# In-projection: products 1 and 2 of all sixteen pairs ahead of the rest, on input that is not yet normalised; up-projection: begun pairs in turns, two products in one bank

## The chip, the cores and the metric

One core of a Trainium2 chip runs the kernel. The metric is the device time of one execution in microseconds (us). The kernel before was timed three times: 1247.93, 1248.74 and 1249.16 us, median 1248.74.

## The reference

One layer of an encoder trunk over 1024 tokens of width 1024, all in float32. What matters here is the first step, and that the same kind of product stands at two more places:

```python
h    = rms_norm(x, norm_mix_pre)            # x * rsqrt(mean(x*x)) * gain
proj = h @ w_in                             # 1024 x 1024 by 1024 x 4096
q, k, v, u, gates = split(proj, ...)
...                                         # attention, pooling, gates, W_o, residual
f = conv_gated_ffn(rms_norm(x), w_up, ...)  # rms_norm(x) @ w_up, 1024 x 5632, conv, GELU gate, @ w_down
x = x + rms_norm(f)
```

The root mean square is taken per token, so in `h @ w_in` it may be left out of the product and multiplied in afterwards, one factor for each token (`Rb` in the code); the gain is per channel of the inner dimension and has to be in before.

## The kernel before

**Products.** A float32 operand is split into a high part (rounded to fp32r, a cast on ScalarE, `wh` or a name with `h`) and the rest (a subtraction on VectorE, `wl` or `l`). A product of two split operands takes three matmuls: high by high, high by low, low by high (`mm3`, L82). All matmuls of the projections are 128x128 weights against 128x512 input columns into one bank of PSUM. One product of 512 inner channels is 4 x 3 = 12 matmuls.

**Pairs.** The output columns of a projection are worked in pairs of 128-column blocks: 16 pairs in the in-projection (`IN_PAIRS`), 22 in the up-projection. A pair is a product of a 2x2 matrix of blocks (two column blocks f by two halves of the inner dimension) and a 2x2 matrix of input quadrants (two halves of the inner dimension by two halves t of the tokens). Done directly it takes 8 products; `Pair` (L165) does it by Strassen and Winograd's scheme in 7: p1 and p2, whose sum is the block f=0, t=0, and then p5, p6, p3, p7, p4, which use sums of weights (`s1` to `s4`, on POOL from L204 to L210) and sums of input quadrants (`T1` to `T4`). p1 and p2 use plain weights (`w11`, `w12`) and plain quadrants (`B11`, `B21`), the first token half. The result of p1 (`c1`) is needed again: p6 accumulates on it in the same bank X.

**In-projection.** The first pairs are where the input comes in, is scaled by the gain and split. Pairs 0 and 1 are done directly, 8 products each (L414, 192 matmuls on four gain-scaled quadrants `XR`), and their results are multiplied by `Rb` at eviction (`evict_first`, L446). Meanwhile the sums of squares (`sq`, L424, ScalarE), the reciprocal roots (`scales`), the spread of them over the partitions by four transposes (`spread`, `rps`) and the normalisation of the four quadrants in place (`normalise`, L440) run. Pairs 2 to 15 then take 7 products each from the normalised quadrants. Pairs 4 and 5 are begun early: their p1 and p2 run in the `m` banks, `c1` is kept in SBUF, and their later products are evicted with an add of `c1` on VectorE (L217, L248, L485). In the others p6 adds to p1 in the bank, and the evictions of p1, p5 and p6 are ScalarE copies. The pool path (trailing means on VectorE) runs beside pairs 8 to 11.

**Up-projection.** Pairs 2, 3, 4 are begun early in the `m` banks: p1 to SBUF, p2 evicted with an add (L1158); both go to DRAM (`e_d`) and come back at the pair's turn, where p5, p6 and p4 are evicted with an add of `c1s`. The order of the begun products is written out by hand from L1218 to L1278.

**What sets the order.** Each engine takes its instructions in one order. The code gives it, a scheduler may move an instruction where a priority (`tc.high_priority`) or a hold (`tc.issue_after`) is set; loads are issued by SP, some stores by ScalarE (`sig_d`). PSUM has eight banks: tags X, Y, Z and m, two each.

Of the kernel before, what the change touches and what calls it, by code (L numbers as in the profile page):

```python
# [46 lines left out]
def trunk(ctx, tc, xn, xt, w_first, w_in, cols, gain_pre, bias, w_ao, w_pg, w_po, w_o, gains, w_up, w_dn, out):  # L47
# [20 lines left out]
    g_d = dram.tile([NG, P, S], F32, name="g_d")  # L68
    e_d = dram.tile([2, 3, P, 512], F32, name="e_d")
# [7 lines left out]
    def split(hi, lo, src, eng=None):  # L77
        r = A.copy(hi, src)  # L78
        (eng or V).tensor_tensor(lo, src, hi.bitcast(F32), ALU.subtract)  # L79
        return r  # L80
# [84 lines left out]
    class Pair:  # L165
# [3 lines left out]

        def __init__(self, raw, T, psp, tmp, name, evict, np_=6, eng=G):  # L170
            self.early, self.eng, self.split = False, eng, {}
            self.weights(raw)
            self.T, self.psp, self.tmp, self.name, self.evict, self.np_ = T, psp, tmp, name, evict, np_
# [38 lines left out]
        def p5(self):  # L212
# [3 lines left out]
            if self.early:  # L216
# [4 lines left out]
        def begin(self, w, c1):  # L221


            self.early, self.c1 = True, c1
            w = w.rearrange("p (q k c) -> p q k c", q=2, k=4)
            self.w11, self.w12 = w[:, 0], w[:, 1]

        def p1(self):
            if self.early:
                self.X = self.bank("m")  # L230
# [4 lines left out]
            A.copy(self.c1, self.X)  # L235

        def p2(self):
            Z = self.bank("m" if self.early else "Z")
# [3 lines left out]
        def p6(self):  # L242
# [3 lines left out]
            self.prod(self.X, self.s2, "T2", self.early, "6")  # L246
            if self.early:
# [15 lines left out]
        def p4(self, last):  # L263
            X, c = (self.bank("Z"), self.c7) if last else (self.X, self.c1 if self.early else None)
# [58 lines left out]


    mx = [[], []]


    with ExitStack() as ph:
# [13 lines left out]
        def out_tile(f, dt=F32):  # L342
            return tmp.tile([P, 512], dt, tag="hl", bufs=4, name=f)
# [4 lines left out]

        XR = {(0, 0): two("T1", "XR00")}
        xts = []
        for n, tag in enumerate(("B11h", "B11l", "B21h", "B21l")):
            x2 = Tp.tile([P, 2, D], F32, tag=tag, name=f"x{n}")
            xts += [x2[:, 0], x2[:, 1]]
        XR[1, 0] = two("T2", "XR10")
        sq = Tp.tile([P, D], F32, tag="B22h", name="sq")
        Tp.tile([P, D], F32, tag="B22l", name="b22l")
        XR[0, 1] = two("T3", "XR01")
        XR[1, 1] = two("T4", "XR11")  # L360

# [7 lines left out]
        A.dma_start(gn, gain_pre)  # L369
        for c in (slice(0, 1), slice(1, 2), slice(2, 4)):  # L370
            nc.sync.dma_start(q[0, 0][:, c], xt[0, 0][:, c])
            nc.sync.dma_start(wr[0][:, c], w_first[0][:, c])
        for c in (slice(0, 2), slice(2, 4)):
            nc.sync.dma_start(q[1, 0][:, c], xt[1, 0][:, c])
            nc.sync.dma_start(wr[1][:, c], w_first[1][:, c])
        for n in range(4):
            nc.sync.dma_start(xts[n], xn[n])
        for i in range(2):
            nc.sync.dma_start(q[i, 1], xt[i, 1])
        for n in range(4, 8):  # L380
            nc.sync.dma_start(xts[n], xn[n])
        nc.sync.dma_start(cv, cols)
# [8 lines left out]
        def split_raw(i, j, k):  # L391
            hi, lo = XR[i, j]
            A.activation(hi[:, k], q[i, j][:, k], AF.Identity, scale=gain(i, k))
            V.scalar_tensor_tensor(lo[:, k], q[i, j][:, k], gain(i, k), hi[:, k].bitcast(F32),
                                   ALU.mult, ALU.subtract)

        ws, acc = {}, {}

        def split_first(i, k):

            place = (lambda: tmp.tile([P, 2, 4, P], F32R, tag="o", name="w0s", bufs=4)) if i == 0 else None
            ws[i, k] = split_w(wr[i][:, k].rearrange("p (b c) -> p b c", b=4), f"first{i}{k}", None, place)

        def bank(b, t, tag):
            acc[b, t] = psp.tile([P, 512], F32, tag=tag, name=f"i_{b}{t}")

        def products(bs, t, i, k):


            wh, wl = ws[i, k]  # L410
            th, tl = XR[i, t]
            for p, (w, x) in enumerate(((wh, th), (wh, tl), (wl, th))):
                for b in bs:
                    nc.tensor.matmul(acc[b, t], w[:, b], x[:, k], start=i == k == p == 0,  # L414
                                     stop=i == 1 and k == 3 and p == 2, skip_group_check=True)
# [11 lines left out]
        def spread(j):  # L427
# [6 lines left out]
            Rb[j] = out_tile(f"R{j}")  # L434
# [7 lines left out]
        def evict_first(pi, t):  # L442
            for f in range(2):
                b = IN_PAIRS[pi][f]
                d = half_tile(f"d{b}_{t}")
# [1059 lines left out]
```

## Time and profile before

| | |
|---|---|
| median of three runs | 1248.74 us |
| the profiled execution | 1248.39 us |
| its span on the core | 1246.6 us |
| PE (matmul) busy | 1231.2 us, 99%, 5756 matmuls |
| VectorE (DVE) busy | 939.8 us, 75% |
| ScalarE (ACT) busy | 657.3 us, 53% |
| GpSimd (POOL) busy | 282.9 us, 23% |
| mean granted TensorE clock | 0.999 |

The profiled execution's time lies 1.8 us above its span, and 0.35 us below the median. The share of busy time is taken over the whole span; stages differ. Up to about 100 us the in-projection prepares its input beside its first products; its last p6 is at 323 us; the scores of the attention run from 332 to 460 us, the products behind it up to about 606 us; the up-projection has its last p6 at 1021 us, and the down-projection the rest.

### The profile page before, as it was taken

What the parts mean: (1) busy time and instruction counts of PE and PEld (TensorE: products, weight loads), DVE (VectorE), ACT (ScalarE), POOL (GpSimd) and SP (SyncE); (2) the same over time, 40 slices, a digit from 0 to 9 for tenths busy, and PEclk for the clock granted to TensorE, in tenths of its full rate; (3) what the DMA queues carried; (4) which work ended last, traced back from release to release, by engine and by line L of the source; (5) the groups of instructions that cost most, each with busy time, mean ns of one, the idle gap of its engine ahead of it and who ended that gap; (6) DMA issues with size and microseconds to landing.
All of it is one profiled execution on the core that took longest, in us unless ns stands there. A gap on an engine that the chain in (4) does not pass through costs nothing.

```text
span 1246.6 us, 16208 instructions
## 1 busy us (share of the span) xinstructions
PE 1231.2 (99%) x5756; PEld 1023.7 (82%) x5756; DVE 939.8 (75%) x1503; ACT 657.3 (53%) x1149; POOL 282.9 (23%) x229
## 2 busy tenths in 40 slices
PE   7999999999999999999999999999999999999997
PEld 6888888888889888888788888888888888888886
DVE  5996346876588887756799988666676676899968
ACT  6663345564487774434545555455545555445553
POOL 0004222232255546000003443334334300000000
PEclk9999999999999999999999999999999999999999
DMA  9336024335988746412344333122231216903103
GB/s 355 138 131 231 26 89 184 129 131 188 297 277 269 263 154 242 152 73 86 112 148 153 130 110 126 61 102 73 79 101 56 88 68 221 377 18 101 35 1 136
DMA packets 57329, 178.11 MB, mean 143 GB/s; under 512 B 5344, under 2 KB 5984, under 8 KB 52384
## 3 DMA queue, kind: packets, MB, share of 16 engines
q1 hardware_dynamic: 51264, 164.23, 37.3%
q10 hardware_dynamic: 4752, 8.39, 1.8%
q0 software_dynamic: 1232, 4.46, 0.9%
q8 instruction: 45, 0.74, 0.2%
q14 instruction: 36, 0.29, 0.1%
HBM read 128.30 MB, written 48.76 MB: 142 GB/s over the span
## 4 chain that ended last, share of the span: by engine, by line
PE 89%; DVE 8%; issue 1%; ACT 1%; DMA 0%; DVEq 0%; SPq 0%; ACTq 0%
PE X_u L86 16%; PE X_i L86 12%; PE Y_u L86 9%; PE X L86 7%; PE wops L1063 7%; PE Y_i L86 6%; PE i L414 4%; PE Z_u L86 4%; PE y L86 4%; PE ybp L86 4%; PE Y L86 3%; PE Z_i L86 3%; PE f L863 3%; PE tp L838 2%; PE m_u L86 2%; PE pst L795 2%
## 5 line engine op out<-in xcount | busy, mean ns | idle before, releaser
L1187 DVE SCALAR_TENSOR_TENSOR hc<-hu,cv,hc 128x1022 f32<-128x1022 f32 (+1 forms) x88 | 122.7, 1396 | 27.0 <-ACT hc L1182 26.8
L78 ACT CAST wh_u<-s_u 128x512 fp32r<-128x512 f32 x88 | 54.4, 619 | 92.4 <-PE X_u L86 41.7
L79 DVE TENSOR_TENSOR wl_u<-s_u,wh_u 128x512 fp32r<-128x512 f32 x88 | 66.5, 757 | 30.0 <-ACT wh_u L78 30.0
L79 DVE TENSOR_TENSOR wl_i<-s_i,wh_i 128x512 fp32r<-128x512 f32 x56 | 42.7, 763 | 37.3 <-ACT wh_i L78 37.1
L78 ACT CAST wh_i<-s_i 128x512 fp32r<-128x512 f32 x56 | 34.6, 622 | 59.9 <-PE X_i L86 21.9
L78 ACT CAST wh_u<-wup 128x512 fp32r<-128x512 f32 x60 | 37.3, 622 | 52.3 <-PE Y_u L86 27.3
L1182 ACT ACTIVATE hc<-hu,cv 128x1024 f32<-128x1024 f32 x44 | 54.6, 1244 | 12.2 <-DVE hu L1131 11.4
L208 POOL TENSOR_TENSOR s_u<-s_u,wup 128x512 f32<-128x512 f32 x19 | 26.6, 1403 | 131.1 <-DVE wl_u L79 131.1
L204 POOL TENSOR_TENSOR s_u<-wup 128x512 f32<-128x512 f32 x19 | 33.7, 1775 | 74.7 <-DVE wl_u L79 74.7
L204 POOL TENSOR_TENSOR s_i<-win 128x512 f32<-128x512 f32 x11 | 15.9, 1446 | 150.8 <-DVE wl_i L79 112.8
L817 POOL TENSOR_SCALAR pe<-pe,st 128x640 f32<-128x640 f32 (+4 forms) x58 | 40.3, 699 | 42.2 <-DVE st L815 28.3
L813 ACT ACTIVATE pe<-sm,st 128x640 f32<-128x640 f32 (+2 forms) x64 | 44.3, 694 | 8.1 <-DVE st L811 7.8
L79 DVE TENSOR_TENSOR ptl<-tp,pth 128x512 fp32r<-128x512 f32 (+3 forms) x80 | 43.0, 552 | 7.4 <-ACT pth L78 6.6
L210 POOL TENSOR_TENSOR s_u<-wup 128x512 f32<-128x512 f32 x19 | 40.7, 2141 | 27.2 <-DVE wl_u L79 27.2
L1192 ACT ACTIVATE hc<-hc 128x1024 f32<-128x1024 f32 x22 | 23.4, 1062 | 39.8 <-DVE hc L1187 39.8
L78 ACT CAST pth<-tp 128x512 fp32r<-128x512 f32 (+3 forms) x80 | 36.4, 474 | 14.8 <-PE tp L838 10.5
L86 PE MATMUL ybp<-mx,wh_yb 128*128 128x512 f32 x128 | 43.4, 414 | 0.0
L78 ACT CAST wh_i<-win 128x512 fp32r<-128x512 f32 x38 | 23.4, 622 | 37.4 <-PE X_i L86 22.8
L79 DVE TENSOR_TENSOR wl_u<-wup,wh_u 128x512 fp32r<-128x512 f32 x60 | 42.1, 702 | 0.7
L811 DVE CUSTOM_DVE_ANT_0 sm<-pst,bt 128x640 f32<-128x640 f32 (+2 forms) x64 | 40.5, 651 | 2.7 <-issue 1.5
L863 PE MATMUL f<-ptl,vv 128*128 128x256 f32 x144 | 36.5, 287 | 0.0
L838 PE MATMUL tp<-ident,pe 128*128 128x128 f32 x240 | 36.2, 275 | 0.1
(503 smaller groups left out, 4169.9 us busy)
## 6 DMA issues: line engine op xcount, KB each, us to landing
wup<-in_w_up SPq DMA_DIRECT2D x22, 1024.0 KB, 5.0
win<-in_w_in SPq DMA_DIRECT2D x14, 1024.0 KB, 5.8
g_d<-hc SPq DMA_DIRECT2D x20, 512.0 KB, 2.7
sig_d<-d ACTq DMA_DIRECT2D x32, 256.0 KB, 2.0
a<-g_d SPq DMA_DIRECT2D x8, 1024.0 KB, 10.9
b<-in_w_dn SPq DMA_DIRECT2D x8, 1024.0 KB, 12.3
x<-in_xn SPq DMA_DIRECT2D x8, 512.0 KB, 11.5
v_d<-vt SPq DMA_DIRECT2D x8, 512.0 KB, 3.1
```

The source lines that it names most:

```text
L78: r = A.copy(hi, src)
L79: (eng or V).tensor_tensor(lo, src, hi.bitcast(F32), ALU.subtract)
L86: nc.tensor.matmul(ps, a[i], b[i], start=start and i == 0 and p == 0, stop=stop and i == n - 1 and p == 2, skip_group_check=True,)
L204: self.eng.tensor_tensor(self.s1, self.w21, self.w22, ALU.add)
L210: self.eng.tensor_tensor(self.s3, self.w11, self.w21, ALU.subtract)
L414: nc.tensor.matmul(acc[b, t], w[:, b], x[:, k], start=i == k == p == 0, stop=i == 1 and k == 3 and p == 2, skip_group_check=True)
L813: A.activation(pe[:, :n], sm[:, :n], AF.Exp, scale=-1.0, bias=st[:, 0:1], accum_out=st[:, 1:2])
L838: nc.tensor.transpose(tp[:, c * P:(c + 1) * P], pe[:, b * P:(b + 1) * P], ident)
L863: nc.tensor.matmul(fo, vv[:, kb, e].rearrange("p a d -> p (a d)"), t[:, s], start=s == slots[0] and x == 0, stop=s == slots[-1] and x == 1)
L1063: nc.tensor.matmul(ps[:, 512 * c:512 * c + 512], a[k // 4][:, k % 4, sl], wo[k][b][:, 512 * c:512 * c + 512], start=k == 0 and x == 0, sto ...
L1182: A.activation(c, hu, AF.Identity, scale=cv[:, C_CW + 88 + b:C_CW + 89 + b], bias=cv[:, C_CB + b:C_CB + b + 1])
L1187: V.scalar_tensor_tensor(c[:, n:], hu[:, :S - n], cv[:, w:w + 1], c[:, n:], ALU.mult, ALU.add)
```

## The change

In the in-projection:

- Only two quadrants (first token half) are scaled by the gain and split, un-normalised (`XR` of two), and these are the operands `B11` and `B21` for all pairs.
- The first 96 matmuls are p1 (into banks X X Y Y) and p2 (into Z Z m m) of pairs 0 to 3 together. For pairs 4 to 15, p1 of pair n and p2 of pair n-1 alternate; p2 accumulates on p1 in one bank, and the tags X, Y, Z take turns. All 16 blocks f=0, t=0 are multiplied by `Rb[0]` at eviction, on VectorE.
- Each `c1` is copied out by ScalarE, stored to a new DRAM tensor (`c1_d`, 16 x 256 KB, issued by ScalarE) and loaded again at the pair's turn (by SP) into a single buffer.
- After that all 16 pairs take their other five products. Before p6, VectorE writes `c1` times `Rb[0]` into the X bank (a seed), and p6 accumulates on it, so p5, p6 and p4 are evicted without an add of `c1`. The pool path runs beside pairs 6, 8, 10, 12, the first two attention heads are loaded beside pair 14.
- The sums of squares, roots, spreads, normalisation and the operands `T1` to `T4`, `B22` are spread between the early products.

In the up-projection the order of the begun products becomes u1 p1, u1 p2, u2 p1, u3 p1, u2 p2, u4 p1, u3 p2, u4 p2, each p2 on its p1 in one bank (tags X, Y, X); the evictions of p2 and of their later p5 and p6 are ScalarE copies, and the X bank is seeded by a ScalarE copy.

```diff
 class Pair:
         def p1(self):
             if self.early:
-                self.X = self.bank("m")
+                self.X = self.bank(self.tags[0])
...
-            A.copy(self.c1, self.X)
+            with tc.high_priority() if self.tags != "mm" else nullcontext():
+                A.copy(self.c1, self.X)
 
         def p2(self):
+            if self.tags != "mm":
+                self.prod(self.X, self.w12, "B21", False, "2")
+                self.evict(0, 0, self.X, None)
+                return
             Z = self.bank("m" if self.early else "Z")
...
             if self.early:
                 self.X = self.bank("X")
-            self.prod(self.X, self.s2, "T2", self.early, "6")
-            if self.early:
+            if self.scale is not None:
+                V.tensor_tensor(self.X, self.c1, self.scale, ALU.mult)
+            elif self.seed:
+                A.copy(self.X, self.c1)
+            self.prod(self.X, self.s2, "T2", self.early and not self.seed, "6")
+            if self.early and not self.seed:
                 V.tensor_tensor(self.u2, self.X, self.c1, ALU.add)
             else:
                 A.copy(self.u2, self.X)
...
+        for n in range(5, NP):
+            if n + 3 < NP:
+                load_w12(n + 3)
+            if n == 6:
+                nc.sync.dma_start(q[1, 1], xt[1, 1])
+            p = begin(n)
+            with tc.high_priority():
+                p.prep("1", p.w11)
+            p.p1()
+            keep_p1(n)
+            with tc.high_priority():
+                p.prep("2", p.w12)
+            pairs[n - 1].p2()
+            if n == 9:
+                values()
+            for x in extra.get(n, ()):
+                x()
...
         def ahead(g):
 
-            p = Pair(None, Tu, psu, tmp, f"u{g}", None, 4)
+            p = Pair(None, Tu, psp, tmp, f"u{g}", None, 4)
...
             def evict(f, t, ps, add):
                 d = p.pt("p2")
-                V.tensor_tensor(d, ps, add, ALU.add)
+                A.copy(d, ps)
                 nc.sync.dma_start(e_d[0, g - 2], d)
```

**How the rows move.** In the rows below, `i7` is pair 7 of the in-projection and `u2` pair 2 of the up-projection; `wh_5_i7` and `wl_5_i7` are the high and low weights of its p5.

VectorE in the in-projection's regular stretch, around the turn from pair 6 to pair 7. Before:

```order
L79 TENSOR_TENSOR wl_7_i6_1244<-s3_i6_1124,wh_7_i6_1243 128x512
L485 TENSOR_TENSOR vd8_1204<-Z_i6_1187,p1_i6_1169 128x512
L79 TENSOR_TENSOR wl_5_i7_1270<-s1_i7_1206,wh_5_i7_1269 128x512
L79 TENSOR_TENSOR wl_4_i6_1287<-win6_956,wh_4_i6_1286 128x512
L485 TENSOR_TENSOR vd8_1204<-Y_i6_1128,u2_i6_1208 128x512
L79 TENSOR_TENSOR wl_1_i7_1308<-win7_1061,wh_1_i7_1307 128x512
L485 TENSOR_TENSOR vd9_1259<-X_i6_1168,p5_i6_1129 128x512
L79 TENSOR_TENSOR wl_2_i7_1326<-win7_1061,wh_2_i7_1325 128x512
L79 TENSOR_TENSOR wl_6_i7_1347<-s2_i7_1261,wh_6_i7_1346 128x512
L79 TENSOR_TENSOR wl_3_i7_1364<-s4_i7_1262,wh_3_i7_1363 128x512
```

VectorE at the same turn, now:

```order
L79 TENSOR_TENSOR wl_5_i7_1707<-s1_i7_1640,wh_5_i7_1706 128x512
L254 TENSOR_TENSOR X_i7_1787<-c1b_7_1638,R0_361 128x512
L79 TENSOR_TENSOR wl_4_i6_1724<-win6_1418,wh_4_i6_1723 128x512
L528 TENSOR_TENSOR d8_1_1678<-Y_i6_1596,u2_i6_1642 128x512
L79 TENSOR_TENSOR wl_6_i7_1790<-s2_i7_1698,wh_6_i7_1789 128x512
L528 TENSOR_TENSOR d9_1_1696<-X_i6_1643,p5_i6_1597 128x512
L79 TENSOR_TENSOR wl_3_i7_1807<-s4_i7_1699,wh_3_i7_1806 128x512
```

The splits of the weights of p1 and p2 and the add of p1 and p2 have gone from the turn; the seed (L254) has come, ahead of the split for p6 and behind that for p5.

VectorE at the second set of reciprocal roots (`bc1` is what `spread(1)` transposes). Before:

```order
L440 SCALAR_TENSOR_TENSOR xq10_105<-xq10_105,gn_112,R0_311 128x512
L309 TENSOR_SCALAR rs_a_339<-rs_a_339 128x4
L79 TENSOR_TENSOR B11l_488<-xq00_104,B11h_487 128x1024
L310 TENSOR_TENSOR rst_143<-rst_143,rs_a_339 128x4
L430 COPY bc1_404<-rst_143 128x512
```

VectorE there, now:

```order
L606 TENSOR_TENSOR d14_0_473<-Y_i5_370,R0_361 128x512
L319 TENSOR_TENSOR rs_a_410<-rs_a_410,rs_v_408 128x4
L478 SCALAR_TENSOR_TENSOR xq10_107<-xq10_107,gn_114,R0_361 128x512
L79 TENSOR_TENSOR wl_1_i8_535<-w12_8_363,wh_1_i8_534 128x512
L320 TENSOR_SCALAR rs_a_410<-rs_a_410 128x4
L478 SCALAR_TENSOR_TENSOR xq10_107<-xq10_107,gn_114,R0_361 128x512
L321 TENSOR_TENSOR rst_152<-rst_152,rs_a_410 128x4
L478 SCALAR_TENSOR_TENSOR xq10_107<-xq10_107,gn_114,R0_361 128x512
L79 TENSOR_TENSOR wl_2_i8_554<-w12_8_363,wh_2_i8_553 128x512
L468 COPY bc1_476<-rst_152 128x512
```

The four small steps of the roots now stand between evictions, splits and normalisations of 512 columns each, and `bc1` behind them.

ScalarE at the start of the up-projection. Before:

```order
L235 COPY hu1_1_6035<-m_u1_6055 128x512
L78 CAST B22h_6228<-h2_11_5214 128x1024
L78 CAST wh_1_u2_6069<-w12_2_6038 128x512
L78 CAST wh_2_u2_6087<-w12_2_6038 128x512
L78 CAST T1h_6112<-h2_00_5211 128x1024
```

ScalarE there, now:

```order
L238 COPY hu1_1_6116<-m_u1_6136 128x512
L79 CAST wh_1_u2_6150<-w12_2_6119 128x512
L79 CAST wh_2_u2_6169<-w12_2_6119 128x512
L79 CAST T1h_6193<-h2_00_5292 128x1024
L79 CAST wh_1_u3_6189<-w12_3_6122 128x512
```

The cast of `B22` no longer stands between the copy for pair 1 and the casts of the weights of pair 2; it follows further down, behind the copy of u2's p1.

More of the change, by code (lines that the diff above doesn't have):

```diff
@@ L570, in trunk @@
+        operand("T4", q[1, 0])
+        nxt.p6()
+        nxt.prep("3", nxt.s4)
+        nxt.p3()
+        pair.p7(False)
+        load_win(2)
+        load_win(3)
+        turn(2)
+        third.first()
+        nxt.p7(False)
+        third.sums()
+        pair.p4(False)
+        third.p5()
+        nxt.p4(False)
+        pair, pd = third, None
+        for pi in range(2, NP):
+            fb = IN_PAIRS[pi]
             for n in (pi + 1, pi + 2):
-                if n < len(IN_PAIRS) and n not in raws and pi >= 1 and (pi < 8 or n == pi + 1):
+                if n < NP and n not in raws and (pi < 9 or n == pi + 1):
```

427 lines of the change are left out of this document (195 added, 232 removed).

## The prediction

> **What bounds the kernel now.** I read the page first: the busy times, the granted clock and the chain that ended last.
>
> ```profile
> PE 1231.2 (99%) x5756; PEld 1023.7 (82%) x5756; DVE 939.8 (75%) x1503; ACT 657.3 (53%) x1149; POOL 282.9 (23%) x229
> PEclk9999999999999999999999999999999999999999
> PE 89%; DVE 8%; issue 1%; ACT 1%; DMA 0%; DVEq 0%; SPq 0%; ACTq 0%
> ```
>
> TensorE (PE) is busy for 1231.2 of 1246.6 us at full clock in every slice, so 15.4 us are idle in all. A busy PE need not be at its peak, so I look at a long stretch without a wait, and at stretches where another engine is full. In these rows of the windows view the columns are sum, PE (matmuls), weight loads, DVE, ACT, POOL, clock, DMA share, GB/s.
>
> ```profile
> 58.00:100.00 42.00, 42.00 (x187) 34.80 (x186) 41.71 (x54) 29.02 (x43) 0.01 (x1) 1.00 0.47 167
> 210.00:230.00 20.00, 19.58 (x86) 15.73 (x85) 15.07 (x21) 11.20 (x18) 6.10 (x4) 1.00 0.39 150
> 620.00:640.00 20.00, 20.00 (x89) 16.22 (x88) 19.82 (x26) 12.49 (x19) 0.00 (x0) 1.00 0.21 73
> 660.00:700.00 40.00, 39.11 (x172) 31.78 (x171) 39.85 (x40) 22.19 (x29) 16.85 (x8) 1.00 0.36 125
> 700.00:900.00 200.00, 200.00 (x884) 165.55 (x883) 149.03 (x169) 101.16 (x143) 73.11 (x45) 1.00 0.26 95
> ```
>
> Between 700 and 900 us, 884 matmuls of 512 columns follow each other without a gap: 200 / 884 = 0.2262 us each. A matmul less is 0.226 us less, as long as nothing else is late. DVE is full at 58 to 100 us and from 620 to 700 us; there the margin of what feeds PE is small. Then the waits of PE:
>
> ```profile
> PE i L414 <- ACT w0s L78: 6.7, 1, 6.7
> PE X_u L86 <- ACT wh_u L78: 0.5, 1, 0.5
> PE X_i L86 <- ACT u_i L250: 0.4, 1, 0.4
> PE X_u L86 <- DVE hu L1131: 0.4, 1, 0.4
> PE m_u L86 <- ACT wh_u L78: 0.3, 1, 0.3
> ```
>
> 6.7 us are the first load, 1.6 us are four waits in the two projections, and the rest of the 15.4 us, 7.1 us, lies in shorter gaps and behind the last matmul. So the bound is the number of matmuls; the waits that a change can remove are small.
>
> **The change part by part.**
>
> *Matmuls.* Pairs 0 and 1 took 8 products of 12 matmuls (the 192 of L414), now 7: 2 x 12 = 24 fewer, all of 128x512. All other pairs keep 7 products. 24 x 0.2262 = **5.4 us less**, on the path since PE is never waiting there. The Trainium skill's page TensorE: Matmul & The Clock Gate ("Wait — 56ns, not 53.3ns?") gives 512 columns 215.7 ns once warm; the row's 226 ns is longer and decides, and by the page's figure the term would be 5.2 us.
>
> *The start.* The first 96 matmuls use the same two quadrants, the same loads in the same order, and the same splits as now. I take no change for the 6.7 us and the cold matmuls.
>
> *First spread.* The roots of tokens 0 to 511 are now asked for behind p1 of pair 4 and ten matmuls of p1 of pair 5, at about 36.5 us (PE's own pace from the start). ScalarE has to do ahead of them, in its order: the copies of four `c1` and four issues, the casts for pairs 4 and 5, and four squares. The rows for these:
>
> ```profile
> L424 ACT ACTIVATE sq<-x 128x1024 f32<-128x1024 f32 x8 | 8.5, 1059 | 0.2
> L78 ACT CAST wh_i<-win 128x512 fp32r<-128x512 f32 x7 | 4.4, 623 | 7.1 <-PE i L414 4.2 <-PE X_i L86 2.7
> L440 DVE SCALAR_TENSOR_TENSOR xq<-xq,gn,R 128x512 f32<-128x512 f32 x16 | 11.4, 745 | 3.0 <-ACT R L435 3.0
> L462 DVE TENSOR_TENSOR xq<-xq,xq 128x1024 f32<-128x1024 f32 x8 | 9.5, 1221 | 0.0
> L446 DVE TENSOR_TENSOR d<-i,R 128x512 f32<-128x512 f32 x8 | 5.0, 681 | 0.0
> L430 DVE COPY bc<-rst x2: 427/428/428, 23.6 to 42.1; 128x512 f32<-128x512 f32 x2
> ```
>
> Four squares are 4.2 us by the row (and up to 0.8 us for reading their sums), five copies of 512 columns 3.1 us by the cast's row (same shape, so an upper bound), the four casts 2.5 us. With four issues of stores (an estimate, under 2 us) that is 10 to 12 us from the last split of the input at about 24 us: the root is out at about 35 us, and the small steps and `bc` follow in some 1.5 us. I take a new wait of 0.3 us, between 0 and 1.5.
>
> *Second spread.* Here DVE is in the way: in its new order the small steps of `bc1` stand between five normalisations, three splits and an eviction. Each costs DVE not its duration but the distance to the next; these rows of the timeline show both:
>
> ```profile
> 99.82 0.69 DVE L79 TENSOR_TENSOR wl_i<-win,wh_i 128x512 fp32r<-128x512 f32 x1
> 100.42 0.68 DVE L79 TENSOR_TENSOR wl_i<-s_i,wh_i 128x512 fp32r<-128x512 f32 x1
> 102.48 1.69 DVE L79 TENSOR_TENSOR wl_i<-s_i,wh_i 128x512 fp32r<-128x512 f32 x1 [1.38 <-ACT wh_i L78]
> 104.09 0.68 DVE L217 TENSOR_TENSOR p_i<-Y_i,c 128x512 f32<-128x512 f32 x1
> 104.69 1.46 DVE L79 TENSOR_TENSOR wl_i<-s_i,wh_i 128x512 fp32r<-128x512 f32 x1
> ```
>
> The second starts 0.60 us after the first, whose duration is 0.69. With 0.60 for a subtraction or product of 512 columns and, likewise 0.09 below its duration, 0.66 for a normalisation, `bc1` comes at about 50.9 us, as PE comes to `rps1` (eleven matmuls into p2 of pair 6). I take 0.2 us, between 0 and 2.4 (by whole durations).
>
> *The rest of the early phase.* PE does 28 products, 96 + 24 x 12 matmuls, up to about 99 us and then five products of pairs 0 and 1. DVE from the first normalisation (about 38.5 us) to the split that p6 of pair 1 needs has, counted in its order: 44 ops of 512 columns, 20 normalisations or scalings, 18 sums of 1024 columns (1.13 each, 1.22 - 0.09), 2 splits of the values, one `bc`, 6 small ones: 26.4 + 13.2 + 20.4 + 1.2 + 0.4 + 0.6 = 62.2 us. With some 8 us in which it waits for PE and ACT before 56 us (my own walk through its order), that ends at about 109 us; PE reaches p6 of pair 1 at about 110.1. No wait, with a margin of 1 to 1.5 us. This is the narrowest place of the change.
>
> *Seeds and c1.* DVE gets 16 seeds and 16 products by `Rb[0]`; it loses 12 adds of p1 and p2 and those of pairs 4 and 5. A turn is now 5 products, 5 x 12 x 0.226 = 13.6 us. Counted with the same prices, DVE has 4.8 us between two seeds for pairs 4 to 8, 10.6, 11.7, 7.4, 11.0, 4.4, 7.3 and 14.9 us before the seeds of pairs 9 to 15. The one above 13.6 follows two light ones, so no seed is late. The stores and loads of `c1_d` are 2 x 16 x 256 KB:
>
> ```profile
> sig_d<-d ACTq DMA_DIRECT2D x32, 256.0 KB, 2.0
> win<-in_w_in SPq DMA_DIRECT2D x14, 1024.0 KB, 5.8
> ```
>
> 256 KB land in 2.0 us, a turn is 13.6 us: hidden, also with one buffer. At SP each reload stands ahead of the next `win` (5.8 us); that is asked for a turn or more ahead. If the cover were gone, a late reload costs at most 2.0 us a turn.
>
> *Old waits of the in-projection.* The wait for `u_i` (0.4 us, in 210 to 230 us) is ScalarE's copy that p7 waits for; the copy stays. The pool path, which crowds ScalarE there (11.20 of 20 us), is now spread over twice as many pairs; I take 0.4 us less, between 0 and 0.4.
>
> *Up-projection.* Same number of matmuls. Three places are late there:
>
> ```profile
> 616.55 1.05 ACT L78 CAST B22h<-h 128x1024 fp32r<-128x1024 f32 x1
> 617.51 0.58 ACT L235 COPY hu<-m_u 128x512 f32<-128x512 f32 x1
> 617.98 1.05 ACT L78 CAST B22h<-h 128x1024 fp32r<-128x1024 f32 x1
> 618.93 1.14 ACT L78 CAST wh_u<-w 128x512 fp32r<-128x512 f32 x2
> 619.60 0.50 PE L86 MATMUL m_u<-B11h,wh_u 128*128 128x512 f32 x1 [0.32 <-ACT wh_u L78]
> 682.41 0.68 DVE L1131 TENSOR_TENSOR hu<-X_u,p_u 128x512 f32<-128x512 f32 x1
> 683.14 0.50 PE L86 MATMUL X_u<-T4h,wh_u 128*128 128x512 f32 x1 [0.41 <-DVE hu L1131]
> 688.57 1.68 POOL L210 TENSOR_TENSOR s_u<-wup 128x512 f32<-128x512 f32 x1 [0.63 <-DVE wl_u L79]
> 692.08 0.47 PE L86 MATMUL X_u<-T3h,wh_u 128*128 128x512 f32 x1 [0.48 <-ACT wh_u L78]
> ```
>
> At 619 us the cast for u2 stands behind 2 x 1.05 us of `B22`; in the new order it is in front of them. At 683 us p4 waits for an eviction on a full DVE; three adds of p2 and the first adds of u2 have gone to ScalarE by then, at least 4 x 0.60 = 2.4 us against a wait of 0.4. At 692 us the weights come late through a sum on POOL that waited for DVE (0.63 us), the same relief. The three waits are 0.32 + 0.41 + 0.48 = 1.2 us, and the first matmul behind each takes 0.47 to 0.50 us where one without a wait takes 0.39. I take 1.4 us less, between 0.3 and 2.0 (with the restarts counted). ScalarE has the time: 12.49 of 20 us and 22.19 of 40 us.
>
> *The sum*, from the profiled 1248.4 us: -5.4 (matmuls) + 0.3 + 0.2 (spreads) - 0.4 (old waits) - 1.4 (up-projection) = **1241.7 us**. The median stands 0.35 us above the profiled run: **1242.0**.
>
> **The rivals.**
>
> *DVE is the bound between 56 and 113 us.* For it: 41.71 of 42 us there already, and more to do in it now. Against: the rows' distance of 0.60. If each op cost its whole duration, 62 us became about 70, 12% more on the 53 us from 56 us on: 6.4 us late less 1.4 us of margin = 5.0 us at p6 of pair 1 (a wait at `rps1` is part of it). 1242.0 + 5.0 = **1247.0**; half of it, 1244.5.
>
> *The up-projection keeps its waits* because POOL's sums (1.68 us above) set them: 1.4 us come back, **1243.4**.
>
> *Slower: the turns become bound by DVE.* A turn shrinks from 7 products to 5 (19.0 to 13.6 us) while POOL still does four sums in it. In the rows above two splits beside POOL took 1.69 and 1.46 us, and the eviction between them, with PSUM on one side, 0.68. A seed reads two SBUF operands as the splits do; the add that it replaces read PSUM. POOL's 6.10 us in 20 make about 5.2 us a turn; if each stretches DVE by its whole length, the turns of pairs 9 to 15 hold 15.8, 16.9, 12.6, 16.2, 9.6, 12.5 and 20.1 us against 13.6: the excess adds up to 8.5 us. With the 5 us of the first rival (no margin to start from) that is 1242.0 + 13.5 = **1255.5**. It decides from the point where DVE's turn is above 13.6 us and the seed has no turn in hand; by the rows only a part of POOL's time stretches DVE. The Trainium skill's page GPSIMD Engine Reference (Key points) says that GpSimd shares its SBUF interfaces with VectorE and that instructions with two SBUF inputs contend; the 1.69 against 0.68 agrees.
>
> **How the numbers follow.** Forecast 0.64, the up-projection rival 0.10, the first rival 0.15, slower 0.05, and 0.06 for waits that I have not seen, a third of them large enough to leave no difference. A measurement of this kernel can tell some 0.2%, 2.5 us: faster is below 1246.2, slower above 1251.2. Faster: the forecast, the up-projection rival, two fifths of the first rival and two thirds of the unseen, 0.64 + 0.10 + 0.06 + 0.04 = 0.84. Same: 0.09 + 0.02 = 0.11. Slower: 0.05. The range: below, all these waits gone and none new, 1248.4 - 5.4 - 0.4 - 2.0 = 1240.6, less 0.8 for the lowest run's distance from the median (1247.93 against 1248.74); above, the first rival in nine tenths of its size, 1242.0 + 4.6.
>
> **What would show it.** Right: PE's count is 5732; the waits list has no new entry above 1 us between 30 and 115 us; the windows from 110 to 300 us show DVE below full; PE's waits at 619, 683 and 692 us (some 6 us earlier) are gone. Wrong: a wait of PE for `seed` or `wl_i` near 110 us, or DVE full in the turns of pairs 9 to 15.

## The result, and the profile after

The changed kernel takes 1259.71 us in the median of six runs (1258.23 to 1259.93), beside 1248.40 us of the kernel before, also the median of six: the ratio is 1.0089, with a 95% interval of 1.0076 to 1.0102. It is 11.3 us slower, where 1242.0 us was forecast. The profiled execution took 1259.18 us, its span 1257.4 us.

The page of the changed kernel, the engines' busy times, PE's busy tenths in 40 slices, and the shares of the chain that ended last:

```profile
PE 1231.3 (98%) x5732; PEld 1021.9 (81%) x5732; DVE 932.1 (74%) x1497; ACT 663.5 (53%) x1170; POOL 300.5 (24%) x236
...
PE   8999999998899999999999999999999999999997
...
PE 82%; DVE 12%; issue 3%; ACT 2%; DMA 2%; SPq 0%; DVEq 0%; POOL 0%; ACTq 0%
```

The 24 matmuls are gone (5732), and yet PE is busy for as long as before. The digits show the place: the tenth and eleventh slice of 40, 283 to 346 us, and nothing behind them. VectorE's and ScalarE's totals have hardly moved, but DVE's share of the chain went from 8% to 12%.

The windows that answer to those shown of before (same columns: sum, PE, weight loads, DVE, ACT, POOL, clock, DMA share, GB/s):

```profile
58.00:100.00 42.00, 42.00 (x191) 34.78 (x190) 41.58 (x56) 27.07 (x41) 0.00 (x0) 1.00 0.75 261
660.00:700.00 40.00, 39.77 (x176) 32.59 (x174) 39.66 (x42) 21.39 (x30) 16.37 (x9) 1.00 0.43 155
```

The early phase runs without a gap on a full DVE, and the up-projection much as it did. So the loss is between 100 and 600 us. This is one stretch in both kernels, the one of before first:

```profile
200.00:340.00 140.00, 139.54 (x618) 114.56 (x617) 99.48 (x150) 74.76 (x131) 37.34 (x35) 1.00 0.54 183
```

```profile
200.00:340.00 140.00, 128.87 (x545) 103.55 (x544) 95.31 (x128) 67.02 (x115) 49.71 (x31) 0.96 0.56 194
```

In 140 us the changed kernel does 73 matmuls fewer: 73 x 0.2262 = 16.5 us lost (taken as if all had 512 columns; 16 of the 618 and 12 of the 545 are shorter). With the 5.4 us of the removed matmuls that is +11.1, against +11.3 measured. Nearly the whole miss lies here, in the turns of the last pairs. The waits of PE in the changed kernel (us in total, times, longest):

```profile
PE first L452 <- ACT w0s L79: 6.3, 1, 6.3
PE Y_i L85 <- ACT wh_i L79: 3.5, 1, 3.5
PE X_i L85 <- DVE d L528: 3.3, 2, 2.7
PE X_i L85 <- ACT u_i L261: 2.5, 2, 2.0
PE vps L542 <- DVE vt L79: 1.1, 1, 1.1
PE X_u L85 <- DVE hu L1148: 1.0, 2, 0.8
PE Y_i L85 <- DVE wl_i L79: 0.8, 1, 0.8
PE rps L471 <- DVE bc L468: 0.2, 1, 0.2
```

`seed` is not among the releasers. What is late are weights (`wh_i`), evictions (`d`, `u_i`) and the transposes of the values (`vps`). In order of time, each as the distance of two matmuls' starts less 0.226:

| | PE stops at (us) | lost (us) | what waits for what |
|---|---|---|---|
| S1 | 213.74 | 1.27 | transposes of the values, for the low part `vt` behind a seed |
| S2 | 234.50 | 2.12 | p7, for ScalarE's copy of p6, behind the pool path's cast |
| S3 | 258.77 | 0.71 | p4, for the eviction of p7 |
| S4 | 285.91 | 0.91 | p5, for its low weights, from a sum on POOL whose input landed late |
| S5 | 302.83 | 2.88 | p4, for the eviction of p7, behind the pool path |
| S6 | 316.82 | 0.67 | p7, for the copy of p6 |
| S7 | 328.54 | 3.70 | p3 of the last pair, for its high weights |

They add up to 12.3 us. The rest of the 16.5 is the clock. Three stretches behind S2, S5 and S7:

```profile
237.20:240.60 3.40, 3.40 (x10) 2.64 (x9) 3.40 (x7) 1.55 (x4) 1.46 (x2) 0.52 0.58 225
306.10:309.50 3.40, 3.40 (x9) 2.69 (x10) 3.40 (x6) 2.30 (x4) 2.05 (x1) 0.57 1.03 333
332.80:336.20 3.40, 3.40 (x9) 2.34 (x8) 1.72 (x3) 1.14 (x3) 0.00 (x0) 0.52 0.86 353
```

3.40 us hold 15 matmuls at full clock and held 28 in three stretches: 45 - 28 = 17 of them are missing, 3.8 us. PE is "busy" all the while, and that is most of why its busy time did not fall with the 24 matmuls.

Now the three large ones. S5 in the timeline (start, duration, engine, line, operation; in brackets the idle time before it and who ended it):

```profile
294.27 2.31 DVE L561 TENSOR_TENSOR pl<-u 128x1023 f32<-128x1023 f32 x1
...
296.50 1.77 DVE L79 TENSOR_TENSOR wl_i<-s_i,wh_i 128x512 fp32r<-128x512 f32 x1
...
298.20 1.25 DVE L560 COPY pl<-pl 128x2 f32<-128x2 f32 x1
...
299.37 1.21 DVE L561 TENSOR_TENSOR pl<-pl 128x1022 f32<-128x1022 f32 x1
299.39 2.34 POOL L209 TENSOR_TENSOR s_i<-win 128x512 f32<-128x512 f32 x1
...
300.11 0.39 PE L85 MATMUL X_i<-T3h,wl_i 128*128 128x512 f32 x1
...
300.50 1.78 DVE L79 TENSOR_TENSOR wl_i<-win,wh_i 128x512 fp32r<-128x512 f32 x1
...
302.27 1.21 DVE L561 TENSOR_TENSOR pl<-pl 128x1020 f32<-128x1020 f32 x1
...
303.40 0.68 DVE L528 TENSOR_TENSOR d<-Y_i,u_i 128x512 f32<-128x512 f32 x1
...
304.07 1.21 DVE L561 TENSOR_TENSOR pl<-pl 128x1016 f32<-128x1016 f32 x1
305.20 0.68 DVE L528 TENSOR_TENSOR d<-X_i,p_i 128x512 f32<-128x512 f32 x1
...
305.94 0.80 PE L85 MATMUL X_i<-T4h,wh_i 128*128 128x512 f32 x1 [2.72 <-DVE d L528]
```

DVE is never idle here, from 293.0 to 311.5 us. `T3` is p7 and `T4` is p4, which goes on in the bank of p7, so that p7's eviction (`d<-X_i,p_i`) has to be out first. p7's last matmul starts at 300.11 and is through by about 300.5, but the eviction starts at 305.20: in between DVE does a split that takes 1.78 us beside a sum on POOL, two additions of the pool path (L561) and the eviction of p3 (`d<-Y_i,u_i`), itself late. Between p7 and p4 PE has only one other product, the next pair's p5, 2.7 us.

Four of these instructions are long because they run beside sums on POOL: the addition at 294.27 (2.31 us, where the others of its kind take 1.21), the splits at 296.50 and 300.50 (1.77 and 1.78 instead of 0.68) and the copy of two columns at 298.20 (1.25 instead of 0.16). That is 4.4 us together on an engine that is never idle, more than the wait of 2.72 us. So two things meet at S5: what stands ahead of the eviction, and how long it takes.

The same chain in the kernel before (its rows between these two left out):

```profile
256.75 0.40 PE L86 MATMUL X_i<-B11h,wh_i 128*128 128x512 f32 x1
256.80 1.22 DVE L531 TENSOR_TENSOR pl<-pl 128x1022 f32<-128x1022 f32 x1
...
265.67 0.68 DVE L485 TENSOR_TENSOR d<-Z_i,p_i 128x512 f32<-128x512 f32 x1
```

It was no shorter, and an eviction stood behind it too. But only its first addition (246.58) stood ahead of the evictions of its turn; the rest began as PE began p1 (`B11`): PE ran on through p1 and p2, 5.4 us that needed none of the evictions then due, and behind them came p6. The change has taken just these two products out of the turn.

S2 is such a chain too, seen on another engine:

```profile
228.37 0.15 DVE L560 COPY pl<-u 128x1 f32<-128x1 f32 x1 [3.04 <-DMA u<-u_d]
...
235.26 1.04 ACT L79 CAST pdh<-pl 128x1024 fp32r<-128x1024 f32 x1 [4.74 <-DVE pl L566]
...
236.21 0.58 ACT L261 COPY u_i<-X_i 128x512 f32<-128x512 f32 x1
...
236.84 0.50 PE L85 MATMUL X_i<-T3h,wh_i 128*128 128x512 f32 x1 [1.96 <-ACT u_i L261]
```

VectorE waits 3.04 us for the pool path's input `u`, the chain's last instruction (L566) starts at 235.08, and ScalarE has stood idle for 4.74 us in front of the cast `pdh`, with the copy of p6 queued behind it. p7 (`T3`) waits for that copy.

S7, first SP's issues in the kernel before, then in the changed one:

```profile
303.72 0.35 SPq L565 DMA_DIRECT2D wr_yb<-in_w_po  x1
...
313.17 1.26 SPq L763 DMA_DIRECT2D qs<-q_d  x1
```

```profile
299.20 0.42 SPq L357 DMA_DIRECT2D qk<-q_d  x1
...
324.26 0.46 SPq L591 DMA_DIRECT2D wr_yb<-in_w_po  x1
...
331.28 0.62 ACT L79 CAST wh_yb<-wr_yb 128x512 fp32r<-128x512 f32 x1 [3.74 <-DMA wr_yb<-in_w_po]
...
332.47 0.50 PE L85 MATMUL Y_i<-B22h,wh_i 128*128 128x512 f32 x1 [3.54 <-ACT wh_i L79]
```

`wr_yb` are the first weights of the pool path's output. Before, SP asked for them 9.45 us ahead of the first attention head, and they landed 2.6 us later. The change puts the loads of two heads (`qk`, `kl`, which wait for stores of `q` and `k`) in front, so that they are asked for at 324.26, land at about 331.2, and ScalarE waits for them with the casts of the last pair's weights behind.

### The profile page after: what moved, and what is told of

Same layout as the page of the kernel before. It is cut to its first block, busy times and chain, and to the rows that moved or that the text cites. A ratio compares the mean times of both kernels' runs of the same rounds, so it can differ in the third digit from the quotient of the medians.

```text
span 1257.4 us, 16281 instructions
## 1 busy us (share of the span) xinstructions
PE 1231.3 (98%) x5732; PEld 1021.9 (81%) x5732; DVE 932.1 (74%) x1497; ACT 663.5 (53%) x1170; POOL 300.5 (24%) x236
## 4 chain that ended last, share of the span: by engine, by line
PE 82%; DVE 12%; issue 3%; ACT 2%; DMA 2%; SPq 0%; DVEq 0%; POOL 0%; ACTq 0%
PE X_u L85 16%; PE X_i L85 10%; PE Y_u L85 8%; PE X L85 7%; PE wops L1080 7%; PE Y_i L85 7%; PE Z_u L85 4%; PE y L85 4%; PE Y L85 3%; PE ybp L85 3%; PE f L881 3%; PE tp L856 2%; PE first L452 2%; PE Z_i L85 2%; DVE hc L1204 1%
## 5 line engine op out<-in xcount | busy, mean ns | idle before, releaser
L1204 DVE SCALAR_TENSOR_TENSOR hc<-hu,cv,hc 128x1022 f32<-128x1022 f32 (+1 forms) x88 | 120.1, 1366 | 30.2 <-ACT hc L1199 29.8
L79 ACT CAST wh_i<-s_i 128x512 fp32r<-128x512 f32 x64 | 39.6, 621 | 73.2 <-PE Y_i L85 21.3
L79 DVE TENSOR_TENSOR wl_i<-s_i,wh_i 128x512 fp32r<-128x512 f32 x64 | 50.2, 791 | 35.5 <-ACT wh_i L79 35.5
L203 POOL TENSOR_TENSOR s_i<-win 128x512 f32<-128x512 f32 x13 | 23.7, 1821 | 174.5 <-DVE wl_i L79 134.9
L203 POOL TENSOR_TENSOR s_u<-wup 128x512 f32<-128x512 f32 x19 | 34.0, 1791 | 72.9 <-DVE wl_u L79 72.9
L881 PE MATMUL f<-pth,vv 128*128 128x256 f32 x144 | 36.5, 286 | 0.0
```

The source lines that it names most:

```text
L79: return A.copy(hi, src), (eng or V).tensor_tensor(lo, src, hi.bitcast(F32), ALU.subtract)
L203: self.eng.tensor_tensor(self.s1, self.w21, self.w22, ALU.add)
L881: nc.tensor.matmul(fo, vv[:, kb, e].rearrange("p a d -> p (a d)"), t[:, s], start=s == slots[0] and x == 0, stop=s == slots[-1] and x == 1)
L1204: V.scalar_tensor_tensor(c[:, n:], hu[:, :S - n], cv[:, w:w + 1], c[:, n:], ALU.mult, ALU.add)
```

## The experiments

**What was to be told apart.** The first theory: the order is at fault. The turn has five products and the pool path's chain stands, in VectorE's and ScalarE's order, ahead of evictions for which PE waits. The rivals: the one buffer for `c1` holds up SP and with it all weights; the loads alone are late (`u`, `wr_yb`); VectorE's capacity in the turns of pairs 9 to 15 is exhausted (the slower rival of the prediction); the up-projection's part costs, not the in-projection's. All ratios are to the kernel before, timed beside each run. In the texts that were written ahead of the runs, theories A and C are the order, rival B is capacity, rival D is weights that land late.

**Two buffers for c1.**

```diff
-            p.c1 = tmp.tile([P, 512], F32, tag="c1", name=f"c1b_{n}", bufs=1)
+            p.c1 = out_tile(f"c1b_{n}")
```

> The changed kernel with two buffers for the reloaded c1 in place of one (the small pool weights get tiles of their own to make room). Theory A (order): the lost time is a few waits in which one late item stands in a queue ahead of what PE needs. Here: the reload of c1 for pair 14 waits in SP's queue for the seed of pair 13, and the weight loads of pairs 13 and 14 stand behind it, so POOL's sums and the splits come late (the waits of 0.9 us at 286 us and 2.9 us at 303 us, with half-clock matmuls behind the second). Then the wait at 286 goes, that at 303 shrinks or goes: 1 to 5 us less, 1255 to 1258.7. Rival B (capacity): VectorE beside POOL has more work than a turn of 13.6 us holds from pair 9 on, so earlier loads only move the waits: within 1 us of 1259.7.

Measured: 1260.17 us, 1.0098 (1.0083 to 1.0113). The waits are those of the changed kernel (3.8 us for `d`, 4.0 for `wh_i`). The buffer is not the cause; one is enough. To make room, the small weights of the pool path (`wgh`, `wgl`) get tiles of their own here, as they do in every later run of the changed kernel except the next one; as this run is no faster, those tiles are not what helps there.

**The pool path's input ahead of the next pair's weights.**

```diff
+            u = None if m is None else pooled_load(m)
             for n in (pi + 1, pi + 2):
                 if n < NP and n not in raws and (pi < 9 or n == pi + 1):
                     load_win(n)
...
-            u = None if m is None else pooled_load(m)
```

> The changed kernel with the load of u for the pool path issued ahead of the weight loads of the same turn. Theory A: at 234.5 us PE waits 2.1 us for ScalarE's copy of u2, which stands behind the cast of the pool path, whose input u landed late, behind weight loads of 1 MB; with the load ahead this wait and the half-clock matmuls behind it go: 2 to 3.5 us less, about 1256.5. Theory B: the wait moves on to the next pool path, within 1 us of 1259.7.

Measured: 1258.86 us, 1.0083 (1.0068 to 1.0098). S2 is gone, but p4 loses 1.5 us for the eviction `d` at 255 us in S3's place (0.7 us there till then), and S7's wait takes 4.3 instead of 3.5. The median is 0.9 us below the changed kernel's, which the two intervals don't tell apart. The late `u` chose the place of a stop; without it, most of the time is lost elsewhere.

**The pool path's output weights ahead of the heads.**

```diff
+            if pi == 13:
+                wr_yb.append(tmp.tile([P, 4, P], F32, name="wr_yb0", bufs=1))
+                nc.sync.dma_start(wr_yb[0], w_po[0])
             if pi == 14:
                 load_head(0)
                 load_head(1)
```

> The changed kernel with the load of the first pool-output weights issued at the end of pair 13, ahead of the loads of the attention heads, into a tile of its own. Theory A: at 328.5 us PE waits 3.7 us for a cast that stands on ScalarE behind the cast of these weights, which landed 7 us after their issue; the wait and the half-clock matmuls behind it go: 4 to 5 us less, about 1255. Theory B (the stretch is full): within 1 us of 1259.7.

Measured: 1252.94 us, 1.0039 (1.0024 to 1.0053), 6.8 us less than the changed kernel. SP issues the load at 53.6 us already, as its tile is free from the start. Its windows:

```profile
300.00:320.00 20.00, 15.61 (x67) 11.97 (x66) 18.17 (x26) 9.23 (x18) 11.74 (x6) 1.00 0.65 210
320.00:340.00 20.00, 20.00 (x93) 16.66 (x92) 12.02 (x25) 9.62 (x19) 4.14 (x12) 1.00 0.97 343
```

S7 is gone (20.00 of 20 us), and so is every stretch of half clock, also behind S2 and S5, which are still there. S7's 3.7 us and the clock's 3.8 are 7.5, less some 2 by which other waits grew (`d` 3.9, `u_i` 2.9, and two new ones of 0.5 and 0.6). That is 5.5; the two profiled executions are 6.2 us apart. So moving this one transfer takes off more than half of the 11.3 us by which the kernel is slower. S7 and the slow stretch behind it, 5.0 us, are shown to hang on it; why the slow stretches behind S2 and S5, 2.5 us, went with it is not shown.

**All three together** (call it the base).

> The three edits together: two c1 buffers, u ahead of the weight loads, the pool-output weights ahead of the heads. Theory A: the gains add up, 8 to 13 us less: 1247 to 1252. Theory B: VectorE stays the bound of the turns, 1257 or more.

Measured: 1251.62 us, 1.0029 (1.0017 to 1.0040). What is left lies between 213 and 316 us, 8.6 us in six stops, the largest S5 with 2.88 as before. These two loads and the buffer are out as causes of what is left, and the kernel is still slower than before.

**The base without the pool path's chain.** VectorE's additions and scalings of the trailing means (L558 to L567) are left out; the loads, the cast and the products stay.

```diff
             src = u
-            step = 1
-            while step < w:
-                dst = tmp.tile([P, S], F32, tag="o", bufs=4, name=f"pl{m}_{step}")
...
-            V.scalar_tensor_tensor(src[:, e:], src[:, e:], 1.0 / w, u[:, e:], ALU.mult, ALU.subtract)
```

> The kernel with the three edits, with the pool path's VectorE chain left out (no trailing means, the split takes u itself; the rest is done). Theory C: what is left are waits behind the pool path on VectorE and ScalarE (1.5 us at 255, 2.9 at 300, 0.7 at 306, 1.2 at 314), so these go and the wait for the split at 283 us (1.0), which comes from late weights, stays: 5 to 6.5 us less than 1251.6, about 1246. Rival D: late weights (two slots for the 1 MB loads from pair 11 on, each free only at the end of a pair) bunch up POOL and VectorE and make the wait at 300 us: then only 2 to 3 us less, about 1249.

Measured: 1244.95 us, 0.9968 (0.9957 to 0.9980). Its waits of PE in the in-projection:

```profile
PE Y_i L85 <- DVE wl_i L79: 0.8, 1, 0.8
PE X_i L85 <- DVE d L528: 0.8, 1, 0.8
```

Against the base, six stops of 8.6 us in all became two of 1.95 in all: 6.6 us, and the time fell by 6.7. So nearly all that was left hung on this chain. Whether it is the chain's place or its length, this run can't tell.

**More buffers for the weights.** The idle buffers of the attention heads hold the weights of pairs 11, 12 and 15, so that the loads of pairs 13 to 15 need not wait for a buffer. The last two are issued 10.0 and 12.5 us earlier than in the base; that of pair 13 is not (275.94 against 275.59).

```diff
-            raws[pi] = raw_tile(f"win{pi}")
+            tag = {11: 'qk0', 12: 'qk1', 15: 'qk1'}.get(pi)
+            raws[pi] = hd.tile([P, 2048], F32, tag=tag, name=f"win{pi}") if tag else raw_tile(f"win{pi}")
```

> The kernel with the three edits, with the weight loads of pairs 11, 12 and 15 in the two 8 KB slots that stand empty between the first stage and the loads of the attention heads, so the loads of pairs 13 to 15 need not wait for the end of the pair before the last. Rival D: the waits at 283 and 300 us and part of those behind them go: 4 to 7 us less than 1251.6, about 1246. Theory C: only the 1.0 us at 283 goes, about 1250.6.

Measured: 1257.99 us, 1.0078 (1.0063 to 1.0093), 6.4 us worse than the base. The stops stay (`d` 5.5 us in three), and the second head, whose buffer is now taken, comes late:

```profile
PE X_i L85 <- DVE d L529: 5.5, 3, 3.8
PE f L886 <- ACT pth L79: 3.9, 1, 3.9
```

A miss. The stop at 284 us stays, as the weights behind it came no earlier. S5 stays with its weights there earlier, and this run says more about it: POOL is idle from 295.9 to 302.7 us, VectorE's instructions from 296.9 to 302.6 have their usual length, and yet the stop grew from 2.71 to 3.76 us. Here p7's eviction stands at 304.91, behind the whole chain, where it stood ahead of the last three steps; these run from 302.53 on. So the place in VectorE's order counts too, not only how full the engine is.

**The pool path at other pairs.** First with these buffers, then on the base alone.

```diff
-            m = {6: 0, 8: 1, 10: 2, 12: 3}.get(pi)
+            m = {6: 0, 8: 1, 9: 2, 10: 3}.get(pi)
...
-            if pi in (7, 11):
+            if pi in (7, 10):
```

> As the one with the slots, and the pool paths beside pairs 6, 8, 9, 10 in place of 6, 8, 10, 12, away from the pairs whose q and k are split on VectorE. Theory C: the waits at 300 to 314 us go (4.8 us), a new one of up to 1.5 us may come at pairs 9 and 10: about 1246. Rival D: same as the kernel with the slots alone, within 1 us.

> The kernel with the three edits, with the pool paths beside pairs 6, 8, 9, 10 in place of 6, 8, 10, 12 and no other slots. The work on VectorE is the same, only its place is another. If the place is the cause (theory C): the waits at 300 to 314 us go, as they did with the slots, and the late second head does not come: 1251.6 less 4 to 5, about 1247. If the amount of work is: within 1 us of 1251.6.

Measured: 1251.41 us, 1.0022 (1.0013 to 1.0032) with the buffers, where the late head still costs 3.7 us; 1246.85 us, 0.9988 (0.9979 to 0.9997) without them. S5 and the stops behind it are gone in both; a wait of 1.7 us for weights has come at 269 us in the second. The same instructions, two of the four chains moved to earlier pairs: 4.8 us less than the base. So the place decides, that is, in which turn a chain stands. The move also takes the chain out of the turn in which VectorE is fullest, and these two runs don't separate that from the order within the turn.

**The values transposed one by one**: what is ready at p6, one tile at p7 and one behind the pair, instead of all at the end of the pair. With the pool path at the other pairs, on the base.

```diff
-        def values():
+        def values(n=4):
 
-            for b, t, d in vds:
+            for b, t, d in vds[:n]:
...
+                     {"p6": values, "p7": lambda: values(1)}, True)
             pair = after
-            values()
+            values(1)
```

> As the one before, with the transposes of the values handed out one by one (behind p6, behind p7 and at the end of a pair) in place of three in a row, for which there are two banks. Theory C: the wait of 1.3 to 1.8 us at 214 us, for the split that frees a bank, goes: 1 to 2 us less, about 1245.5, under the kernel before. Rival: the splits are late because VectorE is, and the wait stays: within 0.5 us of the one before.

Measured: 1245.68 us, 0.9982 (0.9973 to 0.9991). S1 is gone. This is the best complete version, faster than both kernels: 14.0 us below the changed one with all of its work. What it still waits for (the first row is at 61.5 us, the second at 267), and its stretch as a whole:

```profile
PE vps L542 <- DVE d L607: 1.7, 1, 1.7
PE Y_i L85 <- ACT wh_i L79: 1.7, 1, 1.7
...
200.00:340.00 140.00, 137.56 (x624) 113.13 (x623) 106.51 (x161) 75.78 (x135) 49.90 (x42) 1.00 0.62 210
```

VectorE does 106.51 us in these 140, more than in the changed kernel (95.31, which gets less far in them), and PE loses 2.4 us. At 266 us a chain still stands ahead of two evictions. Two stretches from one seed to the next, each with POOL's sums and additions of the pool path (four in the first, three in the second), first S5's in the changed kernel, then one of this version:

```profile
293.00:314.51 21.51, 18.79 (x77) 15.10 (x76) 19.68 (x25) 8.75 (x16) 14.45 (x7) 0.92 0.79 259
```

```profile
214.12:233.54 19.42, 19.38 (x88) 15.69 (x87) 17.32 (x24) 11.48 (x20) 7.65 (x4) 1.00 0.72 258
```

In the second VectorE is busy for 17.32 of 19.42 us and PE does not stop. In the first it is busy for 19.68 of 21.51 us, 4.4 of them from the collisions above, and PE stops at S5.

**The chain's split further back.** In the code of the version above, the cast and the subtraction at the end of the chain (`pdh`, `pdl`) are moved from the chain to p7.

```diff
-            split(hi, lo, src)
-            return m, hi, lo
+            return m, hi, lo, src
...
+            def p7_hook():
+                values(1)
+                if pd is not None:
+                    split(*pd[1:])
```

> As the one before, with the split of the pool path's result behind p7 of the next pair, so that its cast on ScalarE stands behind the copy for p7 and the subtraction nearer to the eviction. Theory C: up to 1 us less than the one before (part of the wait near 270 us); no more, since the chain of sums itself still stands ahead of that eviction.

Measured: 1246.94 us, 0.9988 (0.9979 to 0.9997). The same 1.7 us for `wh_i`, and half clock for some 3.4 us behind it. No gain, but no test of the wait near 270 us either: only the first chain's split moved in the trace (its cast from 202 to 208 us). At the last chain ScalarE and VectorE take the cast, the subtraction and their neighbours in the same order as before the edit, the cast at 266.55 us and 266.80.

**The up-projection's part alone**, on the kernel before.

> The kernel before with the up-projection's part of the change alone (order of the begun products, two products in one bank, ScalarE copies and seeds). The prediction's step: its three waits go, 1.4 us less, 1246.8. What the trace of the changed kernel shows: the first goes, the two at p4 stay or move (0.9, 0.3), so within 0.6 us of 1248.2.

Measured: 1248.36 us, 1.0002 (0.9992 to 1.0011): no change. Its waits there:

```profile
PE X_u L84 <- DVE hu L1141: 1.1, 2, 0.9
```

```profile
695.20 0.50 PE L84 MATMUL X_u<-T4h,wh_u 128*128 128x512 f32 x1 [0.86 <-DVE hu L1141]
```

The first fence is the waits list, the second a row of the timeline. The two waits for weights (0.3 and 0.5 us) are gone; p4's wait for the eviction `hu` was 0.4 and is now 1.1 in two places, 0.86 of it here.

## Why the prediction was wrong

**The steps that held.** *Matmuls:* 5732, and the sum +11.1 needs their full -5.4. *First spread:* 0.2 us at `rps`, forecast 0.3. *Second spread* and *the rest of the early phase:* no wait between 40 and 200 us above 0.4 us, with DVE at 41.58 of 42 us; the first rival (VectorE the bound there) is out. *One buffer for c1:* no loss, and two bring nothing. *"No seed is late":* no run's list has a matmul that waits for one. Four slips in the working leave the forecast as it is: 96 + 24 x 12 matmuls are 32 products, not 28; 18 x 1.13 is 20.3; nine tenths of 5.0 are 4.5; and POOL's row of 6.10 us holds the four sums of a turn, where the slower rival took 5.2.

**The step that failed: "Seeds and c1".** It counted VectorE's work per turn (4.4 to 14.9 us against 13.6) and asked only whether the seed is in time. Over the whole stretch VectorE does have time: in the best version it does more in the same 140 us. In the one turn that was counted above 13.6 the count was too low: 19.7 us measured, 14.9 forecast. And PE waits for single results within a turn. Seven products had p1 and p2 as a place where nothing is due from DVE, and the chain ran there; with five, the same chain stands in VectorE's one order ahead of the evictions of p3 and p7, with one product, 2.7 us, as cover. The rows of VectorE's order quoted ahead of the prediction are of a turn without the pool path; the turn with it is the one that decides.

**"Old waits", -0.4.** I wrote that the pool path is "spread over twice as many pairs" and took relief. The spread is real (from 203.7 to 307.0 us; before, from 200.7 to 264.5), but each pair that holds a chain got it in a shorter turn, and the last chain moved to where POOL is busiest: 12.15 and 11.57 of 20 us from 280 to 320, against 6.70 and 2.74 before. The wait for `u_i` went from 0.4 to 2.5 us. S1 to S6 are 8.6 us, and two runs take most of them off: the base without the chain is 6.7 us below the base, the best version 5.9.

**The loads.** "SP: that is asked for a turn or more ahead" was said of `win` and `c1` alone. The change also moves two heads' loads past `wr_yb`. It was named in the change's description and never priced: 6.8 us with the clock, the most that any one edit to the changed kernel took off. My row of 256 KB in 2.0 us was of stores; this load, in the list of DMA issues from 318 to 334 us, in 7.0:

```profile
wr_yb<-in_w_po SPq DMA_DIRECT2D x1, 256.0 KB, 7.0
```

**Up-projection, -1.4 (0.3 to 2.0).** Measured 0, with an interval that reaches from -1.0 to +1.4 us. I removed three waits by their causes; two went, and their time returned at the next thing that VectorE has to deliver. DVE is as full as before (39.66 of 40 us; 39.85), so what was won at one wait was lost at the next.

**The rivals.** The slower one, given 0.05, had the right place (pairs 9 to 15), the right engine and 1255.5 us. Its mechanism, VectorE's capacity through POOL, was right for one turn: between the last two seeds it gives 20.1 us of work, measured are 19.7; DVE is full there, which the prediction had named as a sign of being wrong, and S5 holds four collisions. It is not the whole: in the six stretches before it, from one seed to the next, DVE had 5.0 to 14.8 us of work in 12.9 to 22.4 us; S2 and S7 came while VectorE or ScalarE stood idle for a load; and the best version has the same sums and the same splits, is 14.0 us faster and keeps PE going through a stretch with 17.32 us of VectorE's work in 19.42. None of the rivals had the half clock.

**The account.** -5.4 (matmuls) + 12.3 (seven stops) + 3.8 (half clock) + 0.4 (small gaps, the rest of the 16.5) is +11.1; measured +11.3. The best version, -2.8 us, stands 3.7 above the forecast: 2.4 us of PE's idle time are left in its stretch, 1.7 are lost at 61.5 us in its profiled execution, and the 1.4 of the up-projection did not come. These are more than 3.7; in the other direction, the half clock at the very start holds for 6 matmuls in this execution and for 12 in the profiled one of the kernel before, some 1.2 us.

**What stays open.** Why the clock fell behind S2 (a wait of 1.96 us) in the changed kernel and not behind S5 (2.72 us) in the run with the pool path's output weights early. The two evictions alone, moved in front of the chain at the same pairs, were not tried: that it matters in which turn a chain stands is shown by moving the chains; how much of S5 is order within the turn and how much is a turn that is simply too full is not. What sets the 1.7 us at 267 us in the best version was not tested.

## What to carry to other kernels

When a turn gets shorter, don't only compare each engine's work with the turn: take the turn with the most side work, and for each result that the busy engine waits for ask what stands ahead of it in its producer's order, and how much cover (here one product, 2.7 us) is left. Price every load that a moved block passes on its queue, the small ones of other stages too. And look at the fullest turn by itself, not at the sum of all: here one turn had 19.7 us of VectorE's work. A wait of two or three microseconds of TensorE can cost nearly half as much again through the clock (here 3.8 us on the 8.7 of three stops), and that part appears as busy time. Last, look in the trace whether an edit has moved what it was to move.

## What the hardware showed that I had not expected

*Half clock behind short waits.* Behind S5 most matmuls of 512 columns start 0.43 us apart (in the window from 306.10 to 309.50, nine in 3.40 us) instead of 0.226. The Trainium skill's page TensorE: Matmul & The Clock Gate (Part 1: The HAM clock gate) describes this: half the clock after an idle window of about 3.4 us, in windows that run freely, 426.7 ns for 512 columns cold. The pitch agrees. The waits of PE here were 1.96, 2.72 and 3.54 us, two of them well below that window; and behind 2.72 us in another run the clock stayed at 1.00. The last two versions show it on one stop: 1.71 us at 267 us in both, with 0.53 us close behind it, full clock after it in the first and half clock in the second. So a wait shorter than the figure may cost a slow window or not, and this case can't say beforehand.

*A seed into PSUM beside POOL.* The product of two SBUF operands that writes a PSUM bank took from 685 to 1791 ns:

```profile
L254 DVE TENSOR_TENSOR X_i<-c1b,R x16: 685/694/1791, 90.2 to 314.5; 128x512 f32<-128x512 f32 x16
```

```profile
212.28 1.75 POOL L209 TENSOR_TENSOR s_i<-win 128x512 f32<-128x512 f32 x1
...
212.80 1.79 DVE L254 TENSOR_TENSOR X_i<-c1b,R 128x512 f32<-128x512 f32 x1
```

The first row is the group (least, median and greatest duration in ns), the others the timeline at S1. This long one ran beside a sum on POOL, and S1 is in the main its consequence: the split `vt` behind it comes 1.1 us late, of 1.27 us lost.
